# Down products of two SwiGLU layers: nine pairs of feature tiles in a seven-product form of halves

## Chip, cores and metric

The kernel runs on one core of one Trainium2 chip. The metric is the device time of one execution in microseconds (us).

## Reference

One step of a two-layer hybrid decoder on 1024 prompt tokens and 32 sample tokens, in float32. Each layer has a mixer and then a feed-forward part (FFN), with a norm ahead of each and one behind it:

```python
def swiglu_ffn(x, w_gate, w_up, w_down):
    return (jax.nn.silu(x @ w_gate) * (x @ w_up)) @ w_down
...
hp = hp + rms_norm(swiglu_ffn(rms_norm(hp, g[2]), ffn_w_gate[layer], ffn_w_up[layer], ffn_w_down[layer]), g[3])
```

The model width is 1024, the hidden width 2816 = 22 feature tiles of 128. The third product, by `w_down`, is the one that the change touches ("down").

## The kernel before

The 1056 tokens lie along the columns, in two halves of 528, or in four quarters of 256, 272, 256 and 272. A product in float32 is made of three matmuls in a reduced format, since both sides are split into a high and a low part: `mm3` (L170 to L173) multiplies high by high (L171), low by high (L172), high by low (L173). A high part is a cast on ScalarE (ACT), a low part a subtraction on GpSimd (POOL) or VectorE (DVE); both inputs of the subtraction lie in SBUF.

`ffn` (from L1114) works on one layer. Its gate and up products go by two hidden tiles at a time and already use seven products of halves in place of eight: `Weights.split` makes the sums of the weights (L1147 to L1154) and their parts (L1140, L1141), `seven` the products. Their results leave PSUM through L1172 (DVE, 128x528) or a copy on ACT, POOL or DVE multiplies gate and up (L1199), and the tile is stored to the DRAM tensor `hd` (L1201, ACT's queue).

The down stage (L1243 to L1305) reads `hd` back. `hids` loads a hidden tile (L1258, SP's queue), ACT casts it (L1259), POOL makes the low part (L1260). `weights` does the same with a tile of `w_down` (L150, L141, L142). Nine chunks of two hidden tiles go by 8 output tiles x 4 quarters; `one` (L1271) runs six matmuls into a PSUM bank and adds the bank to `yacc` (L1281, DVE; in the first chunk a copy on ACT, L1279). The last chunk takes four hidden tiles, one quarter after the other (`LAST_QUARTERS`), and the norm of a token tile (`Tiles`, `Boundary`) runs behind the quarter that it belongs to. A layer has 22 x 8 x 4 x 3 = 2112 down matmuls.

The order of the instructions on each engine, each queue included, is set by a scheduler that simulates the program when it is built. At run time each engine and queue works strictly in that order. Buffers come from pools that open and close with a stage (`Scope`); a tile of a later pool can lie where an earlier tile lay, and then its first writer waits for the last reader there.

Of the kernel before, what the change touches and what calls it, by code (L numbers as in the profile page):

```python
# [2078 lines left out]
```

## Time and profile before

| what | us |
|---|---|
| median of 3 runs | 2861.05 |
| the runs | 2856.1, 2861.05, 2862.39 |
| span of the profiled execution | 2854.8 |
| PE busy in it | 2704.5 (95%) |
| DVE busy in it | 1705.0 (60%) |
| POOL busy in it | 1406.6 (49%) |

The profile is of one execution and gives its span, from its first to its last instruction; the device time of that execution is not given apart. The runs are timed from outside the span, and their median is 6.25 us above it. Busy time leaves out waits, except those that an engine makes inside an instruction.

### The profile page before, as it was taken

The numbers are of one execution on the slowest core, as the hardware profiler recorded it, in microseconds if no ns is written. First come the engines' busy times: TensorE is split into PE (matmuls) and PEld (weight loads), VectorE is DVE, ScalarE is ACT, GpSimd is POOL, SyncE is SP. The second block draws the span as 40 slices with busy tenths as digits, with TensorE's granted clock in tenths as the row PEclk, the third lists the DMA queues.
The fourth block names the chain that finished last, engine by engine and source line by source line (L and its number), as shares of the span: only waits on it lengthen the run. The fifth ranks groups of instructions, "written<-read, shape, count | busy, mean of one in ns | idle before, by whom it ended". The sixth has DMA issues, their size and how long they took to land.

```text
span 2854.8 us, 49751 instructions
## 1 busy us (share of the span) xinstructions
PE 2704.5 (95%) x19508; PEld 2525.9 (88%) x19508; DVE 1705.0 (60%) x3117; ACT 1125.9 (39%) x2053; POOL 1406.6 (49%) x998
## 2 busy tenths in 40 slices
PE   7598998999999999899999999999989999999998
PEld 6587997999999999898888666667989999999998
DVE  8777379755552555733333688885497555543555
ACT  4134364322223211523433677775553222233112
POOL 5954456554556443113553455555465545555440
PEclk9798999999999999999999999999989999999999
DMA  5263362222224222525876655554533221223223
GB/s 147 101 202 109 114 196 96 94 78 77 79 83 147 91 91 76 166 105 169 236 201 175 159 145 145 145 145 130 175 117 98 79 83 65 90 92 104 91 91 130
DMA packets 275662, 350.75 MB, mean 123 GB/s; under 512 B 44056, under 2 KB 208668, under 8 KB 275420
## 3 DMA queue, kind: packets, MB, share of 16 engines
q1 hardware_dynamic: 215252, 289.82, 33.9%
q10 hardware_dynamic: 59024, 53.55, 5.6%
q0 software_dynamic: 1152, 4.19, 0.4%
q8 instruction: 154, 2.52, 0.4%
q14 instruction: 80, 0.66, 0.1%
HBM read 268.29 MB, written 79.39 MB: 122 GB/s over the span
## 4 chain that ended last, share of the span: by engine, by line
PE 79%; DVE 9%; issue 5%; DMA 3%; ACT 2%; POOL 2%; SPq 1%; POOLq 0%; ACTq 0%; DVEq 0%
PE pp L172 9%; PE pp L171 9%; PE pp L173 9%; PE mm L171 7%; PE mm L172 7%; PE mm L173 7%; PE pt L1873 3%; PE s L1839 2%; PE tp L172 2%; PE tp L173 2%; PE tp L171 2%; PE tq L171 2%; PE tq L172 2%; PE tq L173 2%; PE s L1838 2%
## 5 line engine op out<-in xcount | busy, mean ns | idle before, releaser
L171 PE MATMUL pp<-blk,whi 128*128 128x272 f32 (+1 forms) x2240 | 638.2, 287 | 9.3 <-DVE ct L1172 6.7
L172 PE MATMUL pp<-blk,wlo 128*128 128x272 f32 (+1 forms) x2240 | 641.1, 288 | 1.9 <-DVE wlo L1141 1.9
L173 PE MATMUL pp<-blk,whi 128*128 128x272 f32 (+1 forms) x2240 | 638.6, 287 | 0.0
L142 POOL TENSOR_TENSOR wlo<-wraw,whi 128x1024 fp32r<-128x1024 f32 x102 | 246.0, 2420 | 575.4 <-ACT whi L141 552.4
L171 PEld LDWEIGHTS pp<-blk,whi 128*128 128x128 f32 x2240 | 425.5, 191 | 10.7 <-DVE ct L1172 7.1
L172 PEld LDWEIGHTS pp<-blk,wlo 128*128 128x128 f32 x2240 | 425.3, 190 | 2.3 <-DVE wlo L1141 2.3
L173 PEld LDWEIGHTS pp<-blk,whi 128*128 128x128 f32 x2240 | 425.5, 190 | 0.0
L1172 DVE TENSOR_TENSOR c<-pp,c 128x528 f32<-128x528 f32 (+1 forms) x308 | 201.7, 656 | 336.6 <-PE pp L173 331.5
L1141 POOL TENSOR_TENSOR wlo<-S,whi 128x1024 fp32r<-128x1024 f32 x90 | 220.6, 2451 | 361.3 <-ACT whi L1140 361.2
L141 ACT CAST whi<-wraw 128x1024 fp32r<-128x1024 f32 x126 | 131.0, 1053 | 363.9 <-PE mm L173 107.3
L1140 ACT CAST whi<-S 128x1024 fp32r<-128x1024 f32 x100 | 105.0, 1050 | 344.2 <-PE pp L173 313.1
L173 PE MATMUL mm<-hid,whi 128*128 128x256 f32 (+1 forms) x680 | 194.5, 286 | 8.1 <-POOL hid L1260 8.1
L171 PE MATMUL mm<-hid,whi 128*128 128x256 f32 (+1 forms) x680 | 197.9, 291 | 1.8 <-DVE yacc L1281 1.8
L172 PE MATMUL mm<-hid,wlo 128*128 128x256 f32 (+1 forms) x680 | 194.5, 286 | 0.0
L171 PE MATMUL mm<-y,whi 128*128 128x256 f32 (+1 forms) x576 | 167.6, 291 | 0.4 <-DVE s5o L1031 0.4
L173 PE MATMUL mm<-y,whi 128*128 128x256 f32 (+1 forms) x576 | 167.0, 290 | 0.0
L172 PE MATMUL mm<-y,wlo 128*128 128x256 f32 (+1 forms) x576 | 166.7, 289 | 0.0
L1281 DVE TENSOR_TENSOR yacc<-mm,yacc 128x272 f32<-128x272 f32 (+1 forms) x264 | 113.1, 430 | 81.5 <-PE mm L173 81.5
L171 PE MATMUL tp<-hid,whi 128*128 128x272 f32 x484 | 138.3, 287 | 0.0
L172 PE MATMUL tp<-hid,wlo 128*128 128x272 f32 x484 | 138.1, 286 | 0.0
L173 PE MATMUL tp<-hid,whi 128*128 128x272 f32 x484 | 137.6, 285 | 0.0
L173 PEld LDWEIGHTS mm<-hid,whi 128*128 128x128 f32 x680 | 128.6, 189 | 8.9 <-POOL hid L1260 8.9
(516 smaller groups left out, 7684.9 us busy)
## 6 DMA issues: line engine op xcount, KB each, us to landing
wraw<-in_ffn_w_gate_dram SPq DMA_DIRECT2D x52, 512.0 KB
hid<-hd SPq DMA_DIRECT2D x44, 528.0 KB
raw<-in_ffn_w_up_dram SPq DMA_DIRECT2D x44, 512.0 KB
wraw<-in_ffn_w_down_dram SPq DMA_DIRECT2D x44, 512.0 KB
hd<-c ACTq DMA_DIRECT2D x72, 264.0 KB
wraw<-in_ab_w_out_dram SPq DMA_DIRECT2D x24, 512.0 KB
wraw<-in_c_w_qkv_dram ACTq DMA_DIRECT2D x24, 512.0 KB
kt<-in_cache_k_dram SPq DMA_DIRECT2D x32, 384.0 KB
```

Source lines behind the costliest of these rows:

```text
L141: A.copy(hi[:rows], raw[:rows])
L142: lo_eng.tensor_tensor(lo[:rows], raw[:rows], hi[:rows].bitcast(F32), op=sub)
L171: T.matmul(ps, wh, xh, start=start, stop=False)
L172: T.matmul(ps, wl, xh, start=False, stop=False)
L173: T.matmul(ps, wh, xl, start=False, stop=stop)
L1140: A.copy(hi, src)
L1141: (V if early and src is S34 else G).tensor_tensor(lo, src, hi.bitcast(F32), op=sub)
L1172: plus = lambda o, ps, x: V.tensor_tensor(o, ps, x, op=add)
L1281: V.tensor_tensor(yo, ps[:, :n], yo, op=add)
L1838: T.matmul(ps[:, :n], h.qs[:, i * P:(i + 1) * P], h.kh[:, c0:c0 + n], start=True, stop=False)
L1839: T.matmul(ps[:, :n], h.qs[h.own, i * P:(i + 1) * P], h.kl[h.own, c0:c0 + n], start=False, stop=True)
L1873: T.transpose(pt[:, j, r * P:(r + 1) * P], self.u.rows[r].p[:, (self.j0 + j) * P:(self.j0 + j + 1) * P], ident)
```

## The change

Of the 22 hidden tiles, tiles k and k + 9 for k from 0 to 8 make nine pairs. For a pair, the two tiles and the two token halves make four right-hand blocks B11, B12, B21, B22 (128x528), and the two tiles of `w_down` with the two halves of its columns four left-hand blocks A11, A12, A21, A22 (128x512). Seven products of sums of these stand for eight. The sums are S1 to S4 and T1 to T4, all on DVE, and each of the 14 factors needs a high part (ACT) and a low part (8 on POOL, 6 on DVE). The seven products are summed over the pairs in seven tiles Z1 to Z7 (128 x 4 x 528): chunks of two pairs, four full ones and a last one of a single pair; the first chunk copies PSUM to Z on ACT, the others add on DVE (L1344). At the end seven DVE steps on whole Z tiles (`plus`, L1330, 128x2112) put the four quadrants of the result together in Z2, Z3, Z6 and Z7. The last four tiles follow as before, added into these (L1383). Their hidden tiles come from a pool `d3` that is opened after the pool `d2` with Z1, Z4 and Z5 is closed.

The diff, without its changes to comments and without the code for the last four tiles that stays as it is (indented four columns less):

```diff
-    d = Scope(nm("down"), side)
-    d2 = Scope(nm("down"), {"left": "right", "right": "left"}[side])
-    for pool, bufs in ((d.pool, 4), (d2.pool, 2)):
-        for tag in ("hidh", "hidl"):
-            pool.tile([P, NT], F32R, name=nm(tag), tag=tag, bufs=bufs)
-    y = {q: d.pool.tile([P, KT, QUARTERS[q][1]], F32, name=nm("yacc")) for q in LAST_QUARTERS}
...
-    chunks = [range(t, t + 2) for t in range(0, HT - 4, 2)] + [range(HT - 4, HT)]
-    for j, ts in enumerate(chunks):
-        side2 = j == len(chunks) - 2
-        hs = hids(ts, *((d2.pool, 2) if side2 else (d.pool, 4)))
...
-            yo = y[q][:, m]
-            if j == 0:
-                A.copy(yo, ps[:, :n])
-            else:
-                V.tensor_tensor(yo, ps[:, :n], yo, op=add)
-        if len(ts) == 2:
-            for m in range(KT):
-                for q in range(4):
-                    one(m, q, (0, 1))
-            if side2:
-                d2.close()
-            continue
+    other = {"left": "right", "right": "left"}[side]
+    d = Scope(nm("down"), side)
+    d2 = Scope(nm("down"), other)
+    NP = (HT - 4) // 2
+    ORD = ("A11", "B11"), ("A12", "B21"), ("S1", "T1"), ("S2", "T2"), ("S3", "T3"), ("S4", "B22"), ("A22", "T4")
+    Z = {}
+    for j in (2, 6, 3, 7):
+        Z[j] = d.pool.tile([P, 4, HALF], F32, name=nm("Z"))
+    for j in (1, 4, 5):
+        Z[j] = d2.pool.tile([P, 4, HALF], F32, name=nm("Z"))
+    for tag in ("Bh", "Bl"):
+        d2.pool.tile([P, 2 * HALF], F32R, name=nm(tag), tag=tag, bufs=8)
+    d2.pool.tile([P, 2 * HALF], F32, name=nm("tb"), tag="tb", bufs=3)
+    d2.pool.tile([P, 2, DM], F32, name=nm("wr"), tag="wr", bufs=3)
+    def y(q, m):
+        t = Z[{(0, 0): 2, (1, 1): 3, (0, 1): 6, (1, 0): 7}[m // 4, q // 2]]
+        o = q % 2 * 256
+        return t[:, m % 4, o:o + QUARTERS[q][1]]
+    def right_sides(ks):
+        new = lambda n, e: d2.pool.tile([P, len(ks), HALF], F32R, name=nm(n), tag="B" + e, bufs=8)
+        blk = {b: (new(b, "h"), new(b, "l")) for _, b in ORD}
+        raw = {b: blk[b][1].bitcast(F32) for b in ("B11", "B21", "B22")}
+        temp = lambda: d2.pool.tile([P, len(ks), HALF], F32, name=nm("tb"), tag="tb", bufs=3)
+        raw["B12"] = raw["T3"] = temp()
+        for b in ("B11", "B12", "B21", "B22"):
+            for j, k in enumerate(ks):
+                c0 = HALF * (b[2] == "2")
+                nc.sync.dma_start(raw[b][:, j], hd[k + NP * (b[1] == "2")][:, c0:c0 + HALF])
+        def low(b, eng):
+            hi, lo = blk[b]
+            A.copy(hi, raw[b])
+            eng.tensor_tensor(lo, raw[b], hi.bitcast(F32), op=sub)
+        raw["T1"], raw["T2"] = temp(), temp()
+        V.tensor_tensor(raw["T1"], raw["B12"], raw["B11"], op=sub)
+        low("B11", G)
+        V.tensor_tensor(raw["T2"], raw["B22"], raw["T1"], op=sub)
+        V.tensor_tensor(raw["T3"], raw["B22"], raw["B12"], op=sub)
+        low("T1", G)
+        low("T3", V)
+        low("B22", V)
+        raw["T4"] = temp()
+        V.tensor_tensor(raw["T4"], raw["B21"], raw["T2"], op=sub)
+        low("B21", V)
+        low("T2", G)
+        low("T4", G)
+        return blk
+    def left_sides(ks):
+        n = len(ks)
+        r = []
+        for half in range(2):
+            t = d2.pool.tile([P, 2, DM], F32, name=nm("wr"), tag="wr", bufs=3)[:, :n]
+            nc.sync.dma_start(t, dram_ap(w_down, base + (ks[0] + NP * half) * P * DM, [[DM, P], [P * DM, n], [1, DM]]))
+            r.append(t)
+        a11, a21, a12, a22 = (r[i // 2][:, :, i % 2 * 512:i % 2 * 512 + 512] for i in range(4))
+        view = lambda t: t[:, 0:n * 512].rearrange("p (k c) -> p k c", k=n)
+        def low(src, eng):
+            hi, lo = (view(wpool.tile([P, 1024], F32R, name=nm(t), tag=t, bufs=4)) for t in ("whi", "wlo"))
+            A.copy(hi, src)
+            eng.tensor_tensor(lo, src, hi.bitcast(F32), op=sub)
+            return hi, lo
+        s1, s2 = view(wraw()), view(wraw())
+        V.tensor_tensor(s1, a21, a22, op=add)
+        yield low(a11, V)
+        V.tensor_tensor(s2, s1, a11, op=sub)
+        yield low(a12, G)
+        V.tensor_tensor(a21, a11, a21, op=sub)
+        yield low(s1, V)
+        yield low(s2, G)
+        V.tensor_tensor(a12, a12, s2, op=sub)
+        yield low(a21, V)
+        yield low(a12, G)
+        yield low(a22, G)
+    gd = Banks(nm("psumw"))
+    chunks = [range(k, min(k + 2, NP)) for k in range(0, NP, 2)]
+    plus = lambda o, a, b: V.tensor_tensor(Z[o], Z[a], Z[b], op=add)
+    for ci, ks in enumerate(chunks):
+        blk, last = right_sides(ks), ci == len(chunks) - 1
+        for j, (w, (_, bn)) in enumerate(zip(left_sides(ks), ORD), 1):
+            for m in range(4):
+                ps = gd.pool.tile([P, 1024], F32, name=nm("pd"), tag="pp", bufs=4)[:, 256:256 + HALF]
+                ms = slice(m * P, m * P + P)
+                for c in (slice(0, 256), slice(256, HALF)):
+                    for k in range(len(ks)):
+                        mm3(ps[:, c], w[0][:, k, ms], w[1][:, k, ms], blk[bn][0][:, k, c], blk[bn][1][:, k, c],
+                            k == 0, k == len(ks) - 1)
+                if ci == 0:
+                    A.copy(Z[j][:, m], ps)
+                else:
+                    V.tensor_tensor(Z[j][:, m], ps, Z[j][:, m], op=add)
+            if last and j == 2:
+                plus(2, 1, 2)
+            if last and j == 4:
+                plus(1, 1, 4)
+            if last and j == 5:
+                plus(5, 5, 1)
+                plus(7, 7, 5)
+    plus(6, 6, 1)
+    plus(6, 6, 3)
+    plus(3, 3, 5)
+    d2.close()
+    gd.close()
+    Banks(nm("psumd"), mm=2, tp=2, tq=1)
+    d3 = Scope(nm("down"), side)
...
+            hi, lo = (d3.pool.tile([P, NT], F32R, name=nm("hid"), tag=f"hid{e}", bufs=4) for e in "hl")
+            raw = lo.bitcast(F32)
+            nc.sync.dma_start(raw, hd[t])
...
+    ts = range(HT - 4, HT)
+    hs = hids(ts)
...
+        V.tensor_tensor(y(q, m), ps[:, :n], y(q, m), op=add)
```

On DVE the stage starts as follows in the first layer. Before, the rows from the last L1172 on were these (`pp`: PSUM of gate/up, `tq`, `tp`, `mm`: banks of down):

```order
L1172 TENSOR_TENSOR c_9207<-pp_9531,c_9207 128x528
L1172 TENSOR_TENSOR c_9208<-pp_9559,c_9208 128x528
L1281 TENSOR_TENSOR yacc_9606<-tq_9908,yacc_9606 128x256
L1281 TENSOR_TENSOR yacc_9604<-tp_9916,yacc_9604 128x272
L1281 TENSOR_TENSOR yacc_9607<-tp_9924,yacc_9607 128x256
L1281 TENSOR_TENSOR yacc_9605<-mm_9932,yacc_9605 128x272
```

With the change (`tb`: T1 to T4 and B12, `B_1365`: B22 and its parts, `wr`: raw weights, `wraw`: S1 and S2, `wlo`: a low part of a weight block):

```order
L1172 TENSOR_TENSOR c_9207<-pp_9531,c_9207 128x528
L1172 TENSOR_TENSOR c_9208<-pp_9559,c_9208 128x528
L1284 TENSOR_TENSOR tb_9634<-tb_9625,B_1355_9612 128x1056
L1286 TENSOR_TENSOR tb_9635<-B_1365_9622,tb_9634 128x1056
L1287 TENSOR_TENSOR tb_9625<-B_1365_9622,tb_9625 128x1056
L1292 TENSOR_TENSOR tb_9647<-B_1357_9614,tb_9635 128x1056
L1281 TENSOR_TENSOR T_1363_9620<-tb_9625,T_1362_9619 128x1056
L1281 TENSOR_TENSOR B_1365_9622<-B_1365_9622,B_1364_9621 128x1056
L1281 TENSOR_TENSOR B_1357_9614<-B_1357_9614,B_1356_9613 128x1056
L1316 TENSOR_TENSOR wraw_9659<-wr_9655,wr_9657 128x1024
L1312 TENSOR_TENSOR wlo_9663<-wr_9655,whi_9662 128x1024
L1318 TENSOR_TENSOR wraw_9660<-wraw_9659,wr_9655 128x1024
```

Where sums into `yacc` came next, ten steps on SBUF tiles now come first, and the low part of A11 (L1312 `wlo_9663`) is the ninth.

On DVE, the evacuations of products 3 and 4 in the second chunk (`Z_9599` is Z3, `Z_9602` is Z4) have the preparation of the third chunk between them:

```order
L1344 TENSOR_TENSOR Z_9599<-pd_10262,Z_9599 128x528
L1316 TENSOR_TENSOR wraw_10607<-wr_10603,wr_10605 128x1024
L1344 TENSOR_TENSOR Z_9599<-pd_10276,Z_9599 128x528
L1318 TENSOR_TENSOR wraw_10608<-wraw_10607,wr_10603 128x1024
L1320 TENSOR_TENSOR wr_10603<-wr_10603 128x2x512
L1286 TENSOR_TENSOR tb_10583<-B_1493_10570,tb_10582 128x1056
L1287 TENSOR_TENSOR tb_10573<-B_1493_10570,tb_10573 128x1056
L1344 TENSOR_TENSOR Z_9599<-pd_10290,Z_9599 128x528
L1344 TENSOR_TENSOR Z_9599<-pd_10304,Z_9599 128x528
L1344 TENSOR_TENSOR Z_9602<-pd_10322,Z_9602 128x528
L1292 TENSOR_TENSOR tb_10595<-B_1485_10562,tb_10583 128x1056
L1344 TENSOR_TENSOR Z_9602<-pd_10336,Z_9602 128x528
```

In this place the stage had only L1281 rows before, as in the first listing.

At the end of the nine pairs, DVE has these rows (`Z_9600`: Z7, `Z_9598`: Z6, `Z_9597`: Z2, `Z_9601`: Z1, `Z_9603`: Z5):

```order
L1330 TENSOR_TENSOR Z_9600<-Z_9600,Z_9603 128x2112
L1330 TENSOR_TENSOR Z_9598<-Z_9598,Z_9601 128x2112
L1344 TENSOR_TENSOR Z_9600<-pd_11781,Z_9600 128x528
L1344 TENSOR_TENSOR Z_9600<-pd_11789,Z_9600 128x528
L1344 TENSOR_TENSOR Z_9600<-pd_11797,Z_9600 128x528
L1344 TENSOR_TENSOR Z_9600<-pd_11805,Z_9600 128x528
L1330 TENSOR_TENSOR Z_9598<-Z_9598,Z_9599 128x2112
L1330 TENSOR_TENSOR Z_9599<-Z_9599,Z_9603 128x2112
L1383 TENSOR_TENSOR Z_9597<-mm_11880,Z_9597 128x272
L1383 TENSOR_TENSOR Z_9597<-mm_11888,Z_9597 128x272
```

The first sums of the last four tiles (L1383) stand behind all seven sums of Z. On SP's queue, whose order in the first layer's start was

```order
L150 DMA wraw_9618<-in_ffn_w_down_dram 128x1024
L150 DMA wraw_9624<-in_ffn_w_down_dram 128x1024
L150 DMA wraw_9896<-in_ffn_w_down_dram 128x1024
L1258 DMA hid_9609<-hd_4434 128x1056
L1258 DMA hid_9614<-hd_4434 128x1056
L1258 DMA hid_9887<-hd_4434 128x1056
L1258 DMA hid_9892<-hd_4434 128x1056
L150 DMA wraw_9902<-in_ffn_w_down_dram 128x1024
```

it is now

```order
L1276 DMA B_1355_9612<-hd_4434 128x528 x2
L1276 DMA tb_9625<-hd_4434 128x528 x2
L1276 DMA B_1357_9614<-hd_4434 128x528 x2
L1276 DMA B_1365_9622<-hd_4434 128x528 x2
L1304 DMA wr_9655<-in_ffn_w_down_dram 128x2x1024
L1304 DMA wr_9657<-in_ffn_w_down_dram 128x2x1024
L1304 DMA wr_10129<-in_ffn_w_down_dram 128x2x1024
L1276 DMA tb_10099<-hd_4434 128x528 x2
```

The weights of the first chunk stood ahead of the hidden tiles and now stand behind the eight loads of hidden halves (a row `x2` is two of them).

## Rows read from the trace of the kernel before

**Rows 1.** The page: the span, and busy time of each engine, its share and instructions.

```profile
span 2854.8 us, 49751 instructions
...
PE 2704.5 (95%) x19508; PEld 2525.9 (88%) x19508; DVE 1705.0 (60%) x3117; ACT 1125.9 (39%) x2053; POOL 1406.6 (49%) x998
```

**Rows 2.** Windows, down and gate/up: from:to, us, PE PEld DVE ACT POOL, PEclk, DMA, GB/s.

```profile
950.00:1000.00 50.00, 50.00 (x410) 50.00 (x409) 29.45 (x69) 8.32 (x8) 19.26 (x8) 1.00 0.26 86
...
650.00:700.00 50.00, 50.00 (x409) 50.00 (x408) 26.93 (x28) 13.70 (x17) 27.07 (x14) 1.00 0.21 70
```

**Rows 3.** Groups of instructions on PE, down products, first matmul of mm3: busy, mean ns | idle.

```profile
L171 PE MATMUL mm<-hid,whi 128*128 128x256 f32 (+1 forms) x680 | 197.9, 291 | 1.8 <-DVE yacc L1281 1.8
...
L171 PE MATMUL tp<-hid,whi 128*128 128x272 f32 x484 | 138.3, 287 | 0.0
...
L171 PE MATMUL tq<-hid,whi 128*128 128x272 f32 (+1 forms) x244 | 70.2, 288 | 0.0
```

**Rows 4.** Windows of the passage from gate/up to down in the first layer.

```profile
906.00:908.00 2.00, 1.42 (x11) 1.16 (x10) 0.71 (x1) 1.80 (x3) 2.00 (x2) 1.00 1.05 335
...
906.00:922.00 16.00, 11.93 (x80) 11.28 (x80) 0.71 (x1) 8.95 (x17) 16.00 (x9) 0.89 0.75 233
...
914.00:916.00 2.00, 2.00 (x14) 1.81 (x13) 0.00 (x0) 1.90 (x6) 2.00 (x2) 0.81 0.97 180
916.00:918.00 2.00, 2.00 (x11) 2.00 (x11) 0.00 (x0) 0.37 (x1) 2.00 (x2) 0.50 0.73 219
918.00:920.00 2.00, 2.00 (x16) 2.00 (x16) 0.00 (x0) 0.85 (x3) 2.00 (x2) 0.84 0.68 262
```

**Rows 5.** Timeline of the passage (DVE, POOL, ACT queue), and the chain, second layer.

```profile
906.15 0.71 DVE L1172 TENSOR_TENSOR c<-pp,c 128x528 f32<-128x528 f32 x1 [2.25 <-PE pp L173]
...
913.46 1.32 POOL L1199 TENSOR_TENSOR c<-c,c 128x528 f32<-128x528 f32 x1
...
914.81 0.33 ACTq L1201 DMA_DIRECT2D hd<-c  x1
...
2558.43 6.15 DMA hid<-hd
```

**Rows 6.** Single lines: count, ns min/median/max, first and last start, forms.

```profile
L1172 DVE TENSOR_TENSOR c<-pp,c x308: 425/707/709, 494.5 to 2569.4; 128x528 f32<-128x528 f32 x126, 128x272 f32<-128x272 f32 x28
...
L142 POOL TENSOR_TENSOR wlo<-wraw,whi x102: 2341/2403/3288, 270.4 to 2790.6; 128x1024 fp32r<-128x1024 f32 x102
...
L142 DVE TENSOR_TENSOR wlo<-wraw,whi x24: 1206/1226/15684, 28.3 to 2073.1; 128x1024 fp32r<-128x1024 f32 x24
...
L1147 DVE TENSOR_TENSOR S<-wraw,wraw x28: 677/693/1530, 416.5 to 2505.2; 128x512 f32<-128x512 f32 x28
...
L1148 DVE TENSOR_TENSOR S<-S,wraw x28: 665/2780/2798, 418.3 to 2505.9; 128x512 f32<-128x512 f32 x28
```

**Rows 7.** Timeline in gate/up, DVE and POOL; groups of the two-input DVE steps.

```profile
717.88 0.69 DVE L1147 TENSOR_TENSOR S<-wraw,wraw 128x512 f32<-128x512 f32 x1
718.60 2.79 DVE L1148 TENSOR_TENSOR S<-S,wraw 128x512 f32<-128x512 f32 x1
...
718.31 2.54 POOL L1141 TENSOR_TENSOR wlo<-raw,whi 128x1024 fp32r<-128x1024 f32 x1 [0.47 <-ACT whi L1140]
...
L1148 DVE TENSOR_TENSOR S<-S,wraw 128x512 f32<-128x512 f32 x28 | 53.8, 1920 | 0.7
...
L1147 DVE TENSOR_TENSOR S<-raw 128x512 f32<-128x512 f32 x22 | 43.9, 1997 | 0.2
...
L1154 DVE TENSOR_TENSOR S<-wraw,S 128x512 f32<-128x512 f32 x28 | 38.2, 1365 | 0.0
```

**Rows 8.** The hidden tiles of down: ACT cast and POOL low part.

```profile
L1259 ACT CAST hid<-hid x44: 1070/1078/1086, 901.2 to 2768.4; 128x1056 fp32r<-128x1056 f32 x44
...
L1260 POOL TENSOR_TENSOR hid<-hid,hid x44: 2412/2466/2489, 906.3 to 2771.9; 128x1056 fp32r<-128x1056 f32 x44
```

**Rows 9.** Groups of the down evacuations on DVE.

```profile
L1281 DVE TENSOR_TENSOR yacc<-mm,yacc 128x272 f32<-128x272 f32 (+1 forms) x264 | 113.1, 430 | 81.5 <-PE mm L173 81.5
```

More of the change, by code (lines that the diff above doesn't have):

```diff
@@ L1242, in ffn @@
         Y.close()
-        Banks(nm("psumd"), mm=2, tp=2, tq=1)
-        d = Scope(nm("down"), side)
-        d2 = Scope(nm("down"), {"left": "right", "right": "left"}[side])
-        for pool, bufs in ((d.pool, 4), (d2.pool, 2)):
-            for tag in ("hidh", "hidl"):
-                pool.tile([P, NT], F32R, name=nm(tag), tag=tag, bufs=bufs)
-        y = {q: d.pool.tile([P, KT, QUARTERS[q][1]], F32, name=nm("yacc")) for q in LAST_QUARTERS}
-        def hids(ts, pool, bufs):
+        other = {"left": "right", "right": "left"}[side]
@@ L1254, in hids @@
+        plus(6, 6, 1)
[3 more added lines that the diff above has]
+        gd.close()
+        Banks(nm("psumd"), mm=2, tp=2, tq=1)
+        d3 = Scope(nm("down"), side)
+        def hids(ts):
             out = []
             for t in ts:
-                hi, lo = (pool.tile([P, NT], F32R, name=nm("hid"), tag=f"hid{e}", bufs=bufs) for e in "hl")
+                hi, lo = (d3.pool.tile([P, NT], F32R, name=nm("hid"), tag=f"hid{e}", bufs=4) for e in "hl")
                 raw = lo.bitcast(F32)
@@ L1264, in ffn @@
         banks[-1].kinds = "mmqpp"
-        chunks = [range(t, t + 2) for t in range(0, HT - 4, 2)] + [range(HT - 4, HT)]
-        for j, ts in enumerate(chunks):
-            side2 = j == len(chunks) - 2
-            hs = hids(ts, *((d2.pool, 2) if side2 else (d.pool, 4)))
-            ws = [weights(dram_ap(w_down, base + t * P * DM, [[DM, P], [P, KT], [1, P]])) for t in ts]
-            def one(m, q, us):
-                n0, n = QUARTERS[q]
-                ps = linbank()
-                for e, u in enumerate(us):
-                    mm3(ps[:, :n], ws[u][0][:, m], ws[u][1][:, m], hs[u][0][:, n0:n0 + n], hs[u][1][:, n0:n0 + n],
-                        e == 0, e == len(us) - 1)
-                yo = y[q][:, m]
-                if j == 0:
-                    A.copy(yo, ps[:, :n])
-                else:
-                    V.tensor_tensor(yo, ps[:, :n], yo, op=add)
-            if len(ts) == 2:
-                for m in range(KT):
-                    for q in range(4):
-                        one(m, q, (0, 1))
-                if side2:
-                    d2.close()
-                continue
-            tiles = Tiles(after())
-            for e, q in enumerate(LAST_QUARTERS):
-                if e == 1:
-                    banks[-1].kinds = ""
-                for us in ((0, 1), (2, 3)) if e == 0 else ((0, 1, 2, 3),):
-                    for m in range(KT):
-                        one(m, q, us)
-                for i in range(2):
-                    tiles(2 * q + i, lambda k, q=q, i=i: y[q][:, k, i * P:(i + 1) * P])
-                if e == 1:
-                    ys = norm().tile([P, KT, NB * TS], F32, name=nm("ysm"), tag="ysm", bufs=1)
-                    for h in range(2):
-                        A.copy(ys[:, :, 16 * h:16 * h + 16], y[2 * h + 1][:, :, 256:272])
-                    tiles(8, lambda k: ys[:, k])
-            tiles.flush()
@@ new lines, in ffn, with one @@
+        ts = range(HT - 4, HT)
+        hs = hids(ts)
+        ws = [weights(dram_ap(w_down, base + t * P * DM, [[DM, P], [P, KT], [1, P]])) for t in ts]
+        def one(m, q, us):
+            n0, n = QUARTERS[q]
+            ps = linbank()
+            for e, u in enumerate(us):
+                mm3(ps[:, :n], ws[u][0][:, m], ws[u][1][:, m], hs[u][0][:, n0:n0 + n], hs[u][1][:, n0:n0 + n],
+                    e == 0, e == len(us) - 1)
+            V.tensor_tensor(y(q, m), ps[:, :n], y(q, m), op=add)
@@ new lines, in ffn @@
+        tiles = Tiles(after())
+        for e, q in enumerate(LAST_QUARTERS):
+            if e == 1:
+                banks[-1].kinds = ""
+            for us in ((0, 1), (2, 3)) if e == 0 else ((0, 1, 2, 3),):
+                for m in range(KT):
+                    one(m, q, us)
+            for i in range(2):
+                tiles(2 * q + i, lambda k, q=q, i=i: y(q, k)[:, i * P:(i + 1) * P])
+            if e == 1:
+                ys = norm().tile([P, KT, NB * TS], F32, name=nm("ysm"), tag="ysm", bufs=1)
+                for h in range(2):
+                    for mh in range(2):
+                        src = Z[{(0, 0): 2, (1, 1): 3, (0, 1): 6, (1, 0): 7}[mh, h]]
+                        A.copy(ys[:, 4 * mh:4 * mh + 4, 16 * h:16 * h + 16], src[:, :, 512:528])
+                tiles(8, lambda k: ys[:, k])
@@ L1305, in ffn @@
+        tiles.flush()
+        d3.close()
         d.close()
```

## Prediction

> **What bounds the kernel now.** I read the page's busy shares first [rows 1]: TensorE (PE) is busy 95% of the span, VectorE (DVE) 60%, GpSimd (POOL) 49%. A busy PE need not be a full one, so I went to windows of the stages that matter [rows 2]. In the down stage 50 us hold 410 matmuls at the full clock; in the gate and up products, which have the seven-product form already, 50 us hold 409. Both give 50/409 = 0.122 us a matmul, and PE is busy throughout: there the matmul count sets the time. DVE does 29.5 of 50 us in the down stage and 27 in the other. The reader should take two things from this: a matmul saved in the middle of the stage is worth 0.122 us, as long as DVE and the loads keep up; and nothing of it says what the ends of the stage cost. So I read the passage from gate/up to down next [rows 4, 5].
>
> **What is removed.** The page's groups give 680 + 484 + 244 = 1408 matmuls of the down products for each of the three kinds of mm3 [rows 3], 4224 in all, 2112 a layer, 96 for each feature tile. Eighteen tiles are 1728. Nine pairs in the new form are 9 x 7 products x 4 row tiles x 2 column pieces x 3 = 1512. That is 216 fewer a layer, 216 x 0.122 = 26.4 us, **52.7 us** for both, and it is the most that the change can gain. The mean number of columns stays (256 and 272).
>
> **The start of the stage.** Before, the stage is entered at 906.15, when the last gate/up result is taken out of PSUM [rows 5]. From 906 to 922 PE runs 80 matmuls, where 16/0.122 = 131 would fit: 51 x 0.122 = 6.2 us lost, the half clock after the pause included [rows 4].
> After, the first product needs one DVE step, the low part of A11 (L1312), and in DVE's order eight steps stand ahead of it: T1, T2, T3, T4, three low parts, s1. T2 needs both halves of B22. The buffer of its second half is that of the last hidden tile, so its load waits until that tile is stored: take out (0.71), POOL multiply 1.32, issue 0.33 [rows 5], then a store and a load of 264 KB each, together taken as the 6.15 us that the chain of waits shows for a hidden load among others [rows 5]: about T + 8, counted from the end of the last matmul. Behind it in SP's queue stand the loads of 1 MB for the weights, at some 290 GB/s (between the 233 and 335 of two windows [rows 4]) 3.6 us each; s1 needs two of them: T + 15. DVE in the meantime does T2, T3, T4 and three low parts, six of 1.24 us (the 128x1024 low part takes 1.206 [rows 6], three hundredths more for 1056), done at T + 15.5 too. With s1 and the low part, 2 x 1.21, PE starts in earnest at T + 18; only four matmuls can go ahead of that. After a pause the clock was 0.81, 0.50 and 0.84 of full in three windows of 2 us [rows 4]: 2 x (0.19 + 0.50 + 0.16) = 1.7 us. 18 + 1.7 - 6.2 = 13.5, taken as **+14 a layer**. From below: if store and load take 3 us and the loads run together at the best rate, 8; from above, if POOL's low parts stop DVE as described next, 22.
>
> **The middle of the stage.** In a full chunk PE has 336 matmuls, 41.0 us. DVE has 28 evacuations at 0.707 and 14 steps with both inputs in SBUF (7 of 1056 columns, 7 of 1024) at 1.24 and 1.21: 19.8 + 8.7 + 8.5 = 36.9 us, if alone. It isn't alone: POOL has eight low parts of 2.4 us [rows 6, 8], 19.4 us. The rows show what that does. The 128x512 sums in SBUF take 0.68 alone, but 2.79 when a POOL low part runs over them [rows 6, 7]: at 718.60 the DVE sum, started 0.3 us after POOL's, ends only after it; the evacuation, one input from PSUM, never takes more than 0.709. Three groups of such steps in gate/up have means of 1.92, 2.00 and 1.37 against 0.68 [rows 7]: about 1.0 too much each. I take 1.0 for each of the eight POOL steps, since one can stop only one DVE step at a time and evacuations run beside it: DVE comes to 36.9 + 8 = 45, 4 us over PE, in the three chunks in which DVE does the evacuations (chunk 0 uses ACT). **+12 a layer.** From below 0: 36.9 is under 41, and four PSUM tiles of slack (4.4 us) can smooth. From above 25: each POOL step costs a good two.
>
> **The end of the stage.** The last chunk is one pair, 168 matmuls, 20.5 us of PE. DVE has 28 evacuations (19.8), one sum of weights (0.65) and the seven sums of Z over 128x2112. No such row exists; from 0.677 at 512 and 1.206 at 1024 columns [rows 6] the slope is 1.03 ns a column, 1.206 + 1088 x 1.03 ns = 2.33 us each, 16.3 us. Together 36.7 us, 16 us more than PE has. The last four tiles add into Z, and all of it waits in DVE's order behind the last sum. In the second layer PE can run five groups of six matmuls ahead (30 x 0.122 = 3.7), until its banks are full: 16.2 - 3.7 + 1.7 of clock + 1 to 3 for POOL = **+16**. In the first layer the buffers of the last four hidden tiles lie on Z tiles: their loads wait for a sum, three of them for the very last one. Then come the load (4 us at the rate above with its queue), ACT's cast 1.08 and POOL's low part 2.46 [rows 8] before the next matmul: 16.2 + 7.5 - 3 + 1.7 + 2 = 24.4, **+25**. From below 10 and 18, if DVE comes to the last chunk with a lead and the sums run faster than the slope; from above 20 and 30. Before, the end had no such gap: the down evacuations take 0.43 each, and idle is spread over waits for PE [rows 9].
>
> Edits with no cost: 134 fewer DVE steps (hidden behind PE in the middle anyway), ACT's casts (14 of about 1.06 in a chunk, 15 of 41 us), fewer low parts of hidden tiles on POOL. Their cover is PE; where it is gone, at both ends, DVE's order is already counted.
>
> **Sum.** -52.7 + 2 x 14 + 2 x 12 + 16 + 25 = +40.3. The page gives the span of the profiled execution, 2854.8, which the rows belong to; the median of the runs is 2861.05, 6.25 us above it, and I put the sum on the median: **2901 us**. 5.7 us (0.2%) is about what a measurement of this kernel tells from no change.
>
> **Rivals.**
> Rival 1, it ends faster: DVE's extra work is covered. The mechanism is DVE's slack in the middle, 41.0 against 36.9: if POOL's steps fall beside evacuations, the middle costs 0 and DVE reaches the last chunk ahead, so that most sums of Z run under PE. For it: in gate/up the same kinds of steps run without a pause of PE [rows 2]. Against: there DVE has 27 us of work in 50. With 8 + 8 at the starts and 10 + 11 at the ends: 2861 - 52.7 + 37 = 2845. It decides below 26 us of waits a layer. A rule of the Trainium skill speaks for more: Perfetto Trace Analysis, section Identifying the Most-Contended Engine, says to improve the engine with the highest occupancy first; here that is PE [rows 1], and by that alone the time would be 2808, which no row bears out at the ends of the stage.
> Rival 2, POOL and DVE take turns in full: each of eight POOL steps costs DVE the 2.79 - 0.68 = 2.1 us of the worst row [rows 7]. DVE needs 36.9 + 16.8 = 53.7 a chunk, 12.7 over PE, in six chunks 76 instead of 24: 2953. For it: the order puts nine such steps between the eight evacuations of products 3 and 4. Against: the means in gate/up are half of that excess. The Trainium skill, SBUF — State Buffer, section Who interferes with whom, has the rule: a DVE instruction with two inputs in SBUF and a GpSimd one that reads SBUF exclude each other for a whole instruction; the 2.79 row agrees, and by it alone, nothing overlapping, the chunk would be 36.9 + 19.4 = 56.3 us.
> Rival 3, the start is nearly as before, since the loads come early: 2 x 9 less, 2883.
> Rival 4, the change doesn't do what it says: the count of matmuls falls but so does their pace, on other columns and other buffers. The additions of 28 + 24 + 41 = 93 would stand alone: 2954. The rows for gate/up, which has tiles of the same 528 columns, speak against it [rows 2].
>
> **How the numbers follow.** Forecast 0.58, rival 1 0.14, rival 2 0.13, rival 3 0.09, rival 4 0.02, and 0.04 for a sum near zero. The parts' half-widths (14 for both starts, 25 for both middles, 10 for the ends) make some 30 together: 2871 to 2931. To leave out no more than 2 in 10 the range reaches part of rivals 1 and 2: 2864 to 2943. Faster by over 0.2%: 0.14; within: 0.04; slower: 0.82.
>
> **What would show it.** Right: windows inside a full chunk hold fewer than 409 matmuls in 50 us with DVE near full; PE pauses of 15 to 20 us at the start waiting for the low parts of the changed kernel on DVE (L1312, L1281); at the end a pause of about 13 (second layer) and 22 (first layer), released by L1383 and by the hidden low part L1368; L1330 at 2.3 us; two-input steps at means of 1.7 to 2.3. Wrong: PE full across the chunks and pauses at both ends under 8 us (rival 1), or DVE full through all chunks with means over 3 (rival 2).

## The result and the profile after

The changed kernel takes 2931.12 us (2927.17 to 2935.23, 4 runs) where the kernel before takes 2859.82 beside it: a ratio of 1.025, 95% interval 1.0236 to 1.0263, or +71 us. The forecast was 2901, range 2864 to 2943, slower at 0.82. The side was right and the time lies in the range; the sum of +40 was too small by 31 us.

The page after, the lines that answer to [rows 1]:

```profile
span 2928.4 us, 48464 instructions
...
PE 2671.8 (91%) x19076; PEld 2489.1 (85%) x19076; DVE 1888.4 (64%) x2983; ACT 1189.7 (41%) x2117; POOL 1438.8 (49%) x1006
```

PE has 33 us less to do and the span is 73.6 us longer. The 432 matmuls are saved, then (19508 - 19076), and more than twice their worth is lost in places where PE stands or runs at half clock. Windows of the first layer show where; the columns are those of [rows 2].

```profile
908.60:936.00 27.40, 6.24 (x29) 5.94 (x30) 21.52 (x13) 11.63 (x12) 16.14 (x7) 0.56 0.63 230
936.00:980.00 44.00, 40.58 (x320) 40.36 (x319) 26.56 (x16) 27.81 (x42) 22.04 (x8) 0.96 0.26 86
980.00:1030.00 50.00, 43.73 (x342) 43.51 (x341) 41.28 (x43) 14.82 (x15) 21.20 (x9) 0.93 0.26 88
1030.00:1080.00 50.00, 43.78 (x349) 43.57 (x348) 41.54 (x44) 14.66 (x15) 21.99 (x9) 0.93 0.22 74
1080.00:1124.00 44.00, 44.00 (x363) 43.90 (x362) 36.47 (x49) 9.81 (x15) 14.48 (x9) 1.00 0.18 49
1124.00:1140.00 16.00, 12.65 (x102) 12.21 (x101) 16.00 (x19) 3.59 (x5) 9.36 (x4) 1.00 0.12 34
1140.00:1175.00 35.00, 18.23 (x113) 17.17 (x112) 23.28 (x25) 6.40 (x7) 16.19 (x6) 0.71 0.52 182
```

A window of PE at full pace holds one matmul in 0.122 us, so what a window loses is its length less 0.122 times its count:

| place, first layer | lost before | lost after | more | forecast |
|---|---|---|---|---|
| start, 908.6 to 936 | 6.2 [rows 4] | 27.4 - 29 x 0.122 = 23.9 | +17.7 | +14 |
| chunk 0, to 980 | 0 | 44 - 320 x 0.122 = 5.0 | | |
| chunks 1 and 2, to 1030 and 1080 | 0 | 8.3 and 7.4 | +20.4 with chunk 0 and 3 | +12 |
| chunk 3, to 1124 | 0 | -0.3 | | |
| end, 1124 to 1175 | 0 | 3.6 + 21.2 | +24.8 | +25 |

In the second layer the same windows give +21.0, +20.5 and +22.1 (forecast 14, 12, 16). All together: 17.7 + 20.4 + 24.8 + 21.0 + 20.5 + 22.1 - 52.7 = +73.8, the span's 73.6. At the start the last gate/up result leaves PSUM at 908.59; this is the forecast's T in the first layer (2605.25 in the second).

The start, timelines of DVE and then POOL (start, us, engine, line, operation, output and inputs):

```profile
916.44 1.86 DVE L1286 TENSOR_TENSOR tb<-B,tb 128x1056 f32<-128x1056 f32 x1 [4.23 <-DMA B<-hd]
...
924.12 3.46 DVE L1316 TENSOR_TENSOR wraw<-wr,wr 128x1024 f32<-128x1024 f32 x1
927.50 3.43 DVE L1312 TENSOR_TENSOR wlo<-wr,whi 128x1024 fp32r<-128x1024 f32 x1
930.85 3.39 DVE L1318 TENSOR_TENSOR wraw<-wraw,wr 128x1024 f32<-128x1024 f32 x1
...
923.58 6.27 POOL L1281 TENSOR_TENSOR T<-tb,T 128x1056 fp32r<-128x1056 f32 x2 [6.39 <-ACT T L1280]
929.81 3.35 POOL L1312 TENSOR_TENSOR wlo<-wr,whi 128x1024 fp32r<-128x1024 f32 x1
```

T2 (L1286) starts at T + 8, as forecast, and s1 (L1316) at T + 15.5. But s1 takes 3.46 us and the low part of A11 (L1312) 3.43 instead of 1.2, each beside one of POOL's low parts: the two engines seem to take turns, which e1 and e8 below test. PE starts in earnest at T + 22, where the forecast had T + 18. In the second layer T3 (L1287) is stretched to 3.46 us as well, and PE starts at T + 25.9.

The middle, DVE and POOL in chunk 1, ACT in chunk 0, and PE's waits of the first layer's stage (us in all, times, longest):

```profile
996.94 3.50 DVE L1320 TENSOR_TENSOR wr<-wr 128x1024 f32<-128x1024 f32 x1
1000.37 3.39 DVE L1286 TENSOR_TENSOR tb<-B,tb 128x1056 f32<-128x1056 f32 x1
1003.68 1.25 DVE L1287 TENSOR_TENSOR tb<-B,tb 128x1056 f32<-128x1056 f32 x1
1004.85 1.92 DVE L1344 TENSOR_TENSOR Z<-pd,Z 128x528 f32<-128x528 f32 x3
...
996.47 2.88 POOL L1281 TENSOR_TENSOR T<-tb,T 128x1056 fp32r<-128x1056 f32 x1 [2.29 <-PE pd L173]
999.33 3.31 POOL L1312 TENSOR_TENSOR wlo<-wr,whi 128x1024 fp32r<-128x1024 f32 x1
...
959.86 1.07 ACT L1280 CAST T<-tb 128x1056 fp32r<-128x1056 f32 x1 [6.07 <-DVE tb L1287]
...
PE pd L171 <- DVE Z L1344: 17.4, 5, 6.3
PE pd L171 <- ACT whi L1311: 15.9, 1, 15.9
PE mm L171 <- ACT hid L1367: 7.5, 1, 7.5
PE mm L171 <- DVE Z L1344: 7.2, 1, 7.2
...
PE pd L171 <- ACT Z L1342: 3.4, 1, 3.4
```

From 995.9 to 1004.85 DVE takes no product out of PSUM: two of the steps in between are 3.50 and 3.39 us long, beside POOL's 2.88 and 3.31. PE fills its four PSUM tiles and stands up to 6.3 us, and then runs at half clock (the window's mean is 0.93, that of 1005 to 1010 alone 0.50). That is the loss of 8 us, once in a chunk. In chunk 0, where ACT takes the products out (L1342), the same steps of DVE act through ACT: its evacuations stand behind the cast of T3, which waits 6.07 us for DVE (L1287), and PE waits 3.4 us for ACT.

The end, first layer (DVE), second layer (DVE, POOL), first layer (SP's queue), and all sums of Z:

```profile
1143.15 7.71 DVE L1330 TENSOR_TENSOR Z<-Z,Z 128x2112 f32<-128x2112 f32 x2
1150.79 2.54 DVE L1344 TENSOR_TENSOR Z<-pd,Z 128x528 f32<-128x528 f32 x4
...
2853.29 9.01 DVE L1330 TENSOR_TENSOR Z<-Z,Z 128x2112 f32<-128x2112 f32 x2
...
2848.65 15.96 POOL L1368 TENSOR_TENSOR hid<-hid,hid 128x1056 fp32r<-128x1056 f32 x4
...
1139.96 19.36 SPq L1366 DMA_DIRECT2D hid<-hd  x4
...
L1330 DVE TENSOR_TENSOR Z<-Z,Z x14: 2342/3300/4510, 1125.6 to 2857.8; 128x2112 f32<-128x2112 f32 x14
```

A sum of Z alone takes 2.34 us (forecast 2.33). Fourteen of them have a median of 3.30: POOL's low parts for the last four tiles run beside them. In the first layer SP issues four loads in 19.36 us, most of which it stands until the sums of Z that they wait for are done. PE's 7.2 us pause, in both layers, ends with L1344: the last four evacuations stand behind two sums of Z, and the first bank of the last four tiles waits for them.

### The profile page after: what moved, and what is told of

Same layout as the page of the kernel before. It is cut to its first block, busy times and chain, and to the rows that moved or that the text cites. A ratio compares the mean times of both kernels' runs of the same rounds, so it can differ in the third digit from the quotient of the medians.

```text
span 2928.4 us, 48464 instructions
## 1 busy us (share of the span) xinstructions
PE 2671.8 (91%) x19076; PEld 2489.1 (85%) x19076; DVE 1888.4 (64%) x2983; ACT 1189.7 (41%) x2117; POOL 1438.8 (49%) x1006
## 5 line engine op out<-in xcount | busy, mean ns | idle before, releaser
L171 PEld LDWEIGHTS pp<-blk,whi 128*128 128x128 f32 x2240 | 426.3, 191 | 10.7 <-DVE ct L1172 9.7
L1172 DVE TENSOR_TENSOR c<-pp,c 128x528 f32<-128x528 f32 (+1 forms) x308 | 202.0, 656 | 339.0 <-PE pp L173 333.9
L142 POOL TENSOR_TENSOR wlo<-wraw,whi 128x1024 fp32r<-128x1024 f32 x66 | 165.9, 2515 | 320.2 <-ACT whi L141 313.2
L171 PE MATMUL pd<-T,whi 128*128 128x256 f32 (+1 forms) x576 | 170.2, 295 | 37.6 <-DVE Z L1344 30.5
L1344 DVE TENSOR_TENSOR Z<-pd,Z 128x528 f32<-128x528 f32 x224 | 149.6, 699 | 41.4 <-PE pd L173 41.2
L172 PE MATMUL pd<-T,wlo 128*128 128x256 f32 (+1 forms) x576 | 167.8, 291 | 0.0
L173 PE MATMUL pd<-T,whi 128*128 128x256 f32 (+1 forms) x576 | 167.6, 291 | 0.0
L171 PE MATMUL pd<-B,whi 128*128 128x256 f32 (+1 forms) x432 | 124.8, 292 | 39.6 <-ACT whi L1311 35.4
L171 PEld LDWEIGHTS pd<-T,whi 128*128 128x128 f32 x576 | 113.2, 197 | 40.0 <-DVE Z L1344 32.3
L1281 POOL TENSOR_TENSOR T<-tb,T 128x1056 fp32r<-128x1056 f32 (+1 forms) x30 | 74.7, 2493 | 137.4 <-ACT T L1280 106.5
L1141 POOL TENSOR_TENSOR wlo<-wraw,whi 128x512 fp32r<-128x512 f32 (+1 forms) x56 | 116.7, 2084 | 38.1 <-ACT whi L1140 38.1
L172 PE MATMUL pd<-B,wlo 128*128 128x256 f32 (+1 forms) x432 | 124.6, 289 | 10.5 <-DVE wlo L1312 10.5
```

The costliest lines, as they stand in the source:

```text
L142: lo_eng.tensor_tensor(lo[:rows], raw[:rows], hi[:rows].bitcast(F32), op=sub)
L171: T.matmul(ps, wh, xh, start=start, stop=False)
L172: T.matmul(ps, wl, xh, start=False, stop=False)
L173: T.matmul(ps, wh, xl, start=False, stop=stop)
L1141: (V if early and src is S34 else G).tensor_tensor(lo, src, hi.bitcast(F32), op=sub)
L1172: plus = lambda o, ps, x: V.tensor_tensor(o, ps, x, op=add)
```

## The experiments

All runs have the kernel before beside them on the same chip; ratios are to it. Its median is 2855 to 2860 us from group to group of runs, so differences in us between groups can be off by 5. e6, e7 and e8 have two runs each.

**POOL's low parts left out** (e1)

```diff
-                eng.tensor_tensor(lo, raw[b], hi.bitcast(F32), op=sub)
+                if eng is V:
+                    eng.tensor_tensor(lo, raw[b], hi.bitcast(F32), op=sub)
+                else:
+                    blk[b] = (hi, hi)
```

(and the same in `left_sides`)

> Leaves out the eight low parts that POOL makes for each chunk of pairs (the high part stands in for them, so the down products of the pairs are not the reference's); DVE, ACT, PE and the loads keep their work. Theory A (POOL's low parts stop DVE's two-input steps, and that stretches the start, the pauses of the chunks and the end): the two-input steps fall to 1.2 us each, PE starts some 4 us earlier in each layer with its second product 4 us earlier too, the pauses of 6.3 us in chunks 1 and 2 fall under 2 us; about 20 us less a layer, 2931 - 40 = 2891. Theory B (the order and the amount of DVE's own steps set it, POOL does not matter): PE starts and pauses as before, 2931 within 10.

2874.84 us, ratio 1.0061 (1.0042 to 1.0079): 56 us less than the change. Windows of the start, of chunk 0 and of chunk 1:

```profile
904.90:932.00 27.10, 10.92 (x62) 10.62 (x63) 19.53 (x17) 15.18 (x18) 1.29 (x1) 0.62 0.75 272
932.00:976.00 44.00, 44.00 (x363) 44.00 (x362) 23.19 (x22) 28.12 (x40) 0.00 (x0) 1.00 0.29 101
976.00:1018.00 42.00, 42.00 (x346) 42.00 (x345) 35.26 (x44) 14.18 (x14) 0.00 (x0) 1.00 0.32 111
```

PE is full: 346 matmuls in 42 us are 0.121 each. The whole loss of the middle is gone, chunk 0's too. The start loses 27.1 - 62 x 0.122 = 19.5 us, 13.3 more than before (14.3 in the second layer), which is the forecast's 14: what the start costs beyond it are the turns. The first layer's end keeps 23 us. Theory B falls; theory A was short by 16 us. It had left pauses of up to 2 us; the windows of chunks 0 and 1 show none, and no half clock.

**Fills in the place of these low parts** (e8)

```diff
-                eng.tensor_tensor(lo, raw[b], hi.bitcast(F32), op=sub)
+                if eng is V:
+                    eng.tensor_tensor(lo, raw[b], hi.bitcast(F32), op=sub)
+                else:
+                    [eng.memset(lo.bitcast(F32), 0.0) for _ in range(2)]
```

(and the same in `left_sides`)

> POOL's eight low parts of a chunk are replaced by fills with a constant, two for each, which read no input (the output is not the reference's: those low parts are zero). POOL is as busy by its fills as their length makes it, but does not read. Theory A, sharpened (DVE with two inputs in SBUF and POOL stop each other only where POOL reads): DVE's two-input steps stay at 1.2 us and the time is that without POOL's steps, 2875 within 8. Theory E (any POOL step stops DVE): the steps are stretched as before by POOL's busy time, over 2900.

2876.5 us, ratio 1.0061 (1.0038 to 1.0084): as without the steps. POOL and DVE at the place in the chunk that stood before:

```profile
985.29 0.99 POOL L1284 MEMSET T<- 128x1056 f32 x1
986.22 0.96 POOL L1318 MEMSET wlo<- 128x1024 f32 x1
...
985.33 1.25 DVE L1289 TENSOR_TENSOR tb<-B,tb 128x1056 f32<-128x1056 f32 x1
986.50 1.25 DVE L1290 TENSOR_TENSOR tb<-B,tb 128x1056 f32<-128x1056 f32 x1
```

DVE's steps with two inputs in SBUF run beside POOL's fills at 1.22 to 1.25 us. So it is the pair of a POOL step that reads SBUF and a DVE step with two SBUF inputs that takes turns; POOL's being busy is not enough. (The fills are shorter, 0.9 us each, and two of them make 1.8 of a low part's 2.4; but fills run beside the whole of both DVE steps shown.)

**The start in another order** (e2)

```diff
-            V.tensor_tensor(s1, a21, a22, op=add)
             yield low(a11, V)
+            V.tensor_tensor(s1, a21, a22, op=add)
...
+            left, first = left_sides(ks), []
+            if ci == 0:
+                first.append(next(left))
+            blk = right_sides(ks)
```

> In the first chunk the weights are loaded ahead of the hidden halves, and the low part of A11 stands first on DVE, ahead of the sums T1 to T4. Theory A (the first product waits only for its place in DVE's order behind eight other steps): PE starts at T + 7 instead of T + 22; some of it comes back as waits for later factors; about 13 us less a layer, 2931 - 26 = 2905. Theory C (the loads set the start: 2 MB of weights and 2 MB of hidden halves must come in first): the start moves by less than 5 us a layer, over 2921.

2931.91 us, ratio 1.0263 (1.0242 to 1.0284): nothing gained. Theory A misses: PE begins at T + 12 instead of T + 22, but after eight matmuls it stops for other factors. Theory C's time came true (over 2921), but its reason did not: the start moves by 10 us, and the second stop, of 8.2 us, is for POOL and not for a load. POOL's timeline, and PE's waits:

```profile
916.34 2.35 POOL L1312 TENSOR_TENSOR wlo<-wr,whi 128x1024 fp32r<-128x1024 f32 x1 [7.74 <-ACT whi L1311]
...
925.43 3.32 POOL L1281 TENSOR_TENSOR B<-B,B 128x1056 fp32r<-128x1056 f32 x1 [1.20 <-DVE tb L1284]
...
PE pd L171 <- ACT B L1280: 12.1, 1, 12.1
PE pd L173 <- POOL B L1281: 8.2, 1, 8.2
```

The low part of B11, which product 1 needs too, is now third on POOL, and waits there for T1 (L1284) on DVE. So the start is not one wait in DVE's order: to put one factor first delays others. That all 14 factors must be made there, in 14 DVE steps of 1.2 us and 8 POOL steps of 2.4, 36 us if none of them overlap, is an estimate; of the 17.7 us more that the start lost, the turns are 4.4 by e1.

**The single pair first** (e3)

```diff
-        chunks = [range(k, min(k + 2, NP)) for k in range(0, NP, 2)]
+        chunks = [range(0, 1)] + [range(k, k + 2) for k in range(1, NP, 2)]
```

> The chunk of a single pair comes first instead of last. Theory A (the end costs what DVE has more to do than PE in the last chunk, 37 against 20.5 us): a full last chunk has 41 us of PE over 36 us of DVE, so the end's loss falls from 25 and 22 us to about 10 (first layer, the loads behind the last sum stay) and 4; the start has half the work in its steps, minus 6; the second chunk is prepared under only 20 us of PE, plus 10. Together about 15 less a layer: 2900. Theory D (the end is set by the waits of the loads and banks, not by DVE's backlog): the end stays, the time is within 10 of 2931.

2928.93 us, ratio 1.0253 (1.0235 to 1.0272): 2 us. Windows of a middle chunk, of the last chunk and of what follows, first layer:

```profile
961.00:1001.00 40.00, 33.74 (x255) 33.52 (x254) 33.09 (x34) 11.28 (x11) 16.01 (x7) 0.87 0.24 81
...
1081.00:1121.00 40.00, 40.00 (x328) 40.00 (x328) 28.63 (x35) 10.26 (x10) 16.44 (x6) 1.00 0.09 28
...
1141.00:1181.00 40.00, 27.80 (x187) 26.74 (x188) 22.58 (x32) 10.46 (x17) 12.51 (x5) 0.79 0.37 134
```

The last full chunk now loses nothing (328 matmuls in 40 us), and the end falls from 24.8 to 18 us: theory A's mechanism in part, but not its 2900. What it had not counted is that four chunks instead of three now prepare a full one, each with its pause (40 - 255 x 0.122 = 8.9). Theory D's time comes true without its reason, since the end did move.

**Z1, Z4, Z5 allotted behind the B tiles** (e4): the two loops that make them change places.

> Z1, Z4 and Z5 are allotted behind the B tiles in the same pool, so that the last four hidden tiles of the first layer lie on B tiles and their loads wait for the sixth product, not for the last sum of Z. Theory A (that wait is 7.5 us of the first layer's end, but DVE's backlog remains): the first layer's end loses some 5 us, 2926. Theory D (the loads set the end): the first layer's end falls by over 12 us, below 2919.

2931.31 us, ratio 1.026 (1.0241 to 1.028): no change, so neither 2926 nor a time below 2919. The hidden tiles come earlier, and PE's wait of 7.5 us for them is gone, but POOL's low parts for them now run beside the sums of Z: in the first layer the median sum rises from 2.71 to 3.51 us and all seven from 21.0 to 25.3, as in the second.

**All low parts on DVE** (e5): `G` becomes `V` in the eight calls of `low`.

> All fourteen low parts of a chunk of pairs on DVE, none on POOL; the output is the reference's. Theory A (turns of POOL and DVE): the two-input steps take 1.2 us each; DVE has 36.9 + 8 x 1.22 = 46.7 us a chunk over 41 us of PE, so the middle loses 6 us in each of two or three chunks instead of 7 to 8 with the half clock, the start loses what it did (more steps, shorter each), the end is the same: 10 to 20 less, 2915. Theory B (DVE's own amount of work is the cause): 8 more steps a chunk make it 10 us a chunk longer, 2931 + 60 = 2990.

2890.49 us, ratio 1.0104 (1.0085 to 1.0122): 41 us less with 8 DVE steps more a chunk, 24 beyond theory A's 2915; B falls. Two chunks, and two steps in a row:

```profile
977.00:1020.00 43.00, 39.52 (x318) 38.71 (x318) 40.63 (x48) 12.36 (x12) 0.00 (x0) 1.00 0.26 93
1020.00:1063.00 43.00, 40.23 (x325) 39.62 (x325) 41.60 (x50) 13.94 (x14) 0.00 (x0) 1.00 0.22 75
...
917.01 1.25 DVE L1287 TENSOR_TENSOR tb<-B,tb 128x1056 f32<-128x1056 f32 x1
918.18 1.25 DVE L1292 TENSOR_TENSOR tb<-B,tb 128x1056 f32<-128x1056 f32 x1
```

A chunk loses 4.2 and 3.4 us and the clock stays at 1.00: PE waits for a PSUM tile of the pairs in seven pauses of at most 1.8 us in this stage. DVE alone is quicker than its rows: steps of 1.25 us start 1.17 apart. So 28 x 0.62 + 22 x 1.15 = 42.7 us, not 46.7.

**The sums of Z left out** (e6): `plus` does nothing.

> Leaves out the seven sums of Z (the output of the FFN is then four of the seven products, not the reference's). Theory A (the end is DVE's backlog in the last chunk plus the load that waits for the last sum): without 16.3 us of sums DVE has 20.5 us for 20.5 of PE; the ends lose 5 us instead of 25 and 22: 2931 - 37 = 2894. Theory D (the loads and low parts of the last four tiles set the end): 2931 - 10 = 2921.

2899.41 us, ratio 1.0142 (1.0119 to 1.0164): 32 us, theory A's 37 nearly. **Both left out** (e7):

> Leaves out POOL's low parts of the pairs and the sums of Z (not the reference's output, for both reasons). If the two costs add: 2875 - 36 = 2839, which is under the kernel before, since only the starts' 13 us a layer stand against the 52.7 us saved. If they cover the same time: over 2860.

2843.48 us, ratio 0.9946 (0.9925 to 0.9967): 88 us less than the change, 56 + 32. The costs add, and without both the saved matmuls show, in a kernel that leaves work out.

**All three costs taken away** (e9): the new order of the products and of the loads, two parts of an edit whose rest is as listed behind it:

```diff
-        ORD = ("A11", "B11"), ("A12", "B21"), ("S1", "T1"), ("S2", "T2"), ("S3", "T3"), ("S4", "B22"), ("A22", "T4")
+        ORD = ("A11", "B11"), ("S1", "T1"), ("S2", "T2"), ("A12", "B21"), ("S3", "T3"), ("S4", "B22"), ("A22", "T4")
...
-            for b in ("B11", "B12", "B21", "B22"):
+            for b in ("B11", "B12", "W", "B21", "B22"):
+                if b == "W":
+                    between()
+                    continue
```

> A version with the output of the reference that takes away all three costs: every low part of the stage on DVE (none on POOL, the last four tiles and their weights too); the single pair first; in each chunk the products in the order in which their factors can be ready, with the weights loaded ahead of B21 and B22; Z1, Z4, Z5 behind the B tiles; each sum of Z as soon as its two Z tiles are done. Theory A (three separate costs: DVE's order at the start, the turns with POOL, DVE's backlog and the waiting loads at the end): start 8 us lost (6 before the change), middle 11, end 6: a layer -26.4 + 2 + 11 + 6 = -7, together 2860 - 15 = 2845. If DVE is now the bound of the whole stage (theory B): 22 x 1.2 + 28 x 0.7 = 46 us a chunk, 5 over PE in four chunks, and the same ends: over 2865.

2861.64 us (12 runs), ratio 1.0017 (1.0006 to 1.0028): 69 us less than the change, and no gain on the kernel before. Windows of start, passage to chunk 1, its pause, the rest, and the end:

```profile
907.60:935.00 27.40, 20.61 (x140) 19.09 (x140) 21.05 (x29) 21.61 (x39) 1.29 (x1) 0.88 0.82 291
935.00:950.00 15.00, 11.15 (x71) 10.71 (x71) 15.00 (x14) 11.84 (x17) 0.00 (x0) 0.77 0.23 75
950.00:980.00 30.00, 26.60 (x194) 26.18 (x193) 29.26 (x35) 8.25 (x9) 0.00 (x0) 0.89 0.37 125
980.00:1120.00 140.00, 135.50 (x1103) 134.04 (x1103) 135.11 (x154) 40.18 (x39) 0.00 (x0) 1.00 0.20 70
1120.00:1135.00 15.00, 11.34 (x65) 10.56 (x65) 13.25 (x17) 5.25 (x5) 0.00 (x0) 0.77 0.84 298
```

Lost are 10.3, 6.3, 6.3, 5.4 and 7.1 us; less the 6.2 of before that is 29 against 26.4 saved. DVE is busy 135 of 140 us: theory B's bound, at a smaller price. **The single pair last again** (e10):

> As e9_all_together, but with the single pair last as in the change. Theory A (the last chunk's sums of Z need PE work to hide under): DVE has 20 + 16 us of evacuations and sums and 9 us of low parts for the last four tiles over 20.5 us of PE in the last chunk: the ends lose some 18 us more a layer than in e9, the start 5 more, the middle 4 less: e9 + 38. Theory D (loads set the ends): within 10 of e9.

2871.97 us, ratio 1.006 (1.0045 to 1.0076): 10 us more, not 38. PE's first wait is 10.7 us instead of 5.7, as expected. The end was priced about right and the middle wrongly, as the trace shows for the first layer: from 1090 to 1136 it holds 195 matmuls and loses 22.2 us, 15 more than e9's end (1095 to 1135, 272 matmuls, 6.8); the start loses 13.3 against 10.3; but the chunks between lose 5 us in all where e9 loses 18, 12.6 of these from 935 to 980. That is 5 us more a layer. Theory D's time (within 10 of e9) is nearly met, but by this offset and not by its reason. **Hidden low parts, and two of a chunk, back on POOL** (e11, e12):

> As e9_all_together, but the low parts of the last four hidden tiles back on POOL, where DVE, full from the last chunk on, has only evacuations beside them. Theory A (the remaining end is DVE's backlog; POOL does not stop evacuations that read PSUM): DVE is freed of 4 x 1.2 us behind the last sum of Z, the ends lose 3 to 4 us less a layer: e9 - 7 = 2855. If the hidden tiles' loads and casts are what is waited for: no change from e9, or 2 us more a layer since POOL takes 2.5 us for one.

> As e11, and of each full chunk the two low parts that are needed last (T4 and A22) back on POOL. Theory A: DVE has 42.8 us a chunk in e9 over 41 us of PE; two steps less make 40.5, but each POOL step stops one DVE step for 1 to 2 us: from 5 us less a layer to 3 more, e11 - 10 to e11 + 6. If the turns cost a whole POOL step each (2.4 us): 4 chunks x 2.4 us more than is saved, e11 + 0 to e11 + 10.

2865.24 us, ratio 1.0022 (1.0013 to 1.0031), and 2870.22, ratio 1.0037 (1.0025 to 1.0049): no gain, then 5 us more, with intervals that overlap. Theory A's 2855 for e11 misses; e12 lies where both of its theories allow it and does not tell them apart. No version that leaves nothing out beats the kernel before.

## Why the prediction was right, and where its sizes were not

All three losses were larger than forecast, by 11 (starts), 17 (middles) and 6 us (ends) by the spans, and 2931 lies at the top of the 2871 to 2931 that the parts' half-widths make. The side was right by its mechanism; the range held with little to spare.

- **What is saved** was right: 52.7 us. The sum closes with it, and e7 shows it.
- **The start** (+14 a layer, measured 17.7 and 21.0). The times of T2 (T + 8) and s1 (T + 15) were right to a microsecond in the first layer. What set s1 there is DVE's order, in which no time is idle from 916.44 on; whether the weights came as late as forecast the trace does not show. The step that failed is "with s1 and the low part, 2 x 1.21": both stood in POOL's turns at 3.4 us, and T3 too in the second layer. It was in the bound from above, where it should have been in the sum, since POOL's steps for the same factors become ready at that moment. Without POOL's steps (e1) the start costs 13.3 and 14.3. e2 shows that this change of order alone is worth nothing while the turns last.
- **The middle** (+12 a layer, measured 20.4 and 20.5) is the term that was mis-sized most, 17 of the 33 us by the spans. The price of a POOL step was near: the 112 two-input steps of the full chunks have a mean of 1.75 us against 1.23 in e1, 7.3 us a chunk where the forecast had 8. The step that failed is "DVE comes to 45, 4 us over PE, in the three chunks": DVE is busy 41.3 us of 50, not all of the time, and PE stands all the same. DVE's steps for the next chunk stand together between the evacuations of products 3 and 4, as the order shows, two of them stretched to 3.4 (the knot, in what follows); PE stops once for up to 6.3 us and pays for it again at half clock. The forecast charged the clock at the ends alone. Nor are its three chunks the ones: it took 1 to 3, where DVE evacuates, but the pauses are in chunks 0, 1 and 2, which prepare a full chunk; chunk 3, with half a preparation, has none. e1 takes all of it away.
- **The end** (+25 and +16, measured 24.8 and 22.1). The price of a sum of Z, 2.33, was right (2.34). The "1 to 3 for POOL" of the second layer was too little: its sums took 25.3 us against 16.3, since POOL's low parts for the last four tiles run beside them, those of the weights first and the hidden ones beside the last two sums. In the first layer three of the four hidden ones cannot, for their loads wait; its sums took 21.0, and PE waits 7.5 us for the tiles instead. So both layers lose nearly the same, and e4 gained nothing. That the first layer's 25 came out so exactly is in part luck: its sums took 4.7 us more than forecast, while evacuations in a row start 0.62 us apart, not 0.707, 2.4 us less for the 28. And the pauses are not the one that was forecast, released by L1383 or L1368: 7.2 us end with L1344, and then come 4.2 for L1383 or 7.5 for the hidden tile's cast (L1367).
- **Rival 1** did not happen; its 2845 is about e7's 2843, in which the turns and the sums are not covered but left out. The rule of the Trainium skill (Perfetto Trace Analysis, Identifying the Most-Contended Engine) would have given 2808 by PE's work alone. The runs do not bear it out here: PE had 33 us less to do, and the kernel became slower.
- **Rival 2** lies between: its 2.1 us for each of eight steps is too much on average (DVE is busy 41 us in a window of 342 matmuls, not 54 in 336), but right for the steps in the knot. The rule of the Trainium skill (SBUF — State Buffer, Who interferes with whom) agrees with e8: POOL steps that only write do not stop DVE's, and evacuations with one SBUF input (L1344) took at most 0.710 us throughout.
- **Rivals 3 and 4** did not happen: the start lost 17.7 and 21.0 us more, and chunk 3 holds 363 matmuls in 44 us, 0.121 each, so the new form keeps the pace.

What stays open: the first matmul after the pause in e9 (950 to 980) still waits for DVE's knot, and whether an order of DVE by need alone, with the evacuations ahead of the preparation, would bring it under the kernel before was not tried; the scheduler sets that order.

## What to carry to other kernels

Matmuls saved are worth their cadence only where the engines that prepare and collect for them keep up in every stretch of a few microseconds, not on average: look at the order of their steps between two evacuations, and add the half clock to a long pause of PE (here it came after 6.3 us, and not with the pauses of at most 1.8 us in e5). Where DVE and POOL both work on SBUF tiles, count their steps with two SBUF inputs as one engine's; here it was faster to give all of them to DVE, 8 steps more in each chunk, than to share them. When three costs cover one saving, take them away one by one and together: the sums must close.
